# Three merge gates of a hybrid encoder layer, computed among the recurrent branch's first products instead of beside attention

## The chip, the cores and the metric

The kernel runs on one core of a Trainium2 chip. Its engines are TensorE (PE, with its weight loads shown as PEld), VectorE (DVE), ScalarE (ACT), GpSimd (POOL) and SyncE (SP), each with an instruction stream of its own; semaphores order them. The metric is device time in microseconds of one execution; the comparison is between medians of several executions of the kernel before and after the change. Profiles are of one execution each.

## The reference

A trunk of two layers over 512 positions of width 1024, in float32. Each layer normalises x, projects it once, feeds three token mixers, and merges them with three sets of sigmoid gates:

```python
for i in range(DEPTH):                       # DEPTH = 2
    h = rmsnorm(x, mix_norm[i])
    z = h @ w_in[i]
    u_rnn, u_gelu, c_q, ckv_rope, fq, fk, fv, f_logit, gate_logit = split_columns(z)
    y_a = rglru_branch(u_rnn, u_gelu, ...) @ w_br_a[i]      # conv, gates, scan, times gelu
    y_b = mla_branch(c_q, ckv_rope, ...) @ w_br_b[i]        # low-rank attention, chunk mask
    y_c = fox_branch(fq, fk, fv, f_logit, ...) @ w_br_c[i]  # attention with cumulative log forget gates
    g = jax.nn.sigmoid(gate_logit + gate_b[i]).reshape(B, S, N_BRANCH, D)
    merged = g[:, :, 0] * y_a + g[:, :, 1] * y_b + g[:, :, 2] * y_c
    x = x + merged @ w_o[i]
    hf = rmsnorm(x, ffn_norm[i]) @ w_gate_up[i]
    x = x + (jax.nn.silu(hf[..., :D_FF]) * hf[..., D_FF:]) @ w_down[i]
    pg = jax.nn.sigmoid(rmsnorm(x, ple_norm[i]) @ w_ple_gate[i])
    x = x + pg * (p[i] @ w_ple[i])
return rmsnorm(x, final_norm)
```

The gate logits of branch n are 1024 columns of z, so 8 blocks of 128 columns for each branch. The change concerns the first three blocks of branch 0, whose gates multiply the recurrent branch's output y_a.

## The kernel before

**Products in three parts.** Activations lie transposed, 128 channels on the partitions and 512 positions along the free dimension. Every float32 operand is split into a high and a low float32r half, and `mm3` (L239) adds three matmuls: high by high, high by low, low by high. `dense` (L246) makes one block of 128 output channels: it takes a PSUM bank, runs `mm3` for each 128-row weight tile (8 for a projection from width 1024, 4 from width 512), and then calls an evacuation function.

**The weight stream.** All weights are packed in the order of use in units of four 128x128 tiles. SP loads a unit into one of four raw slots (`_load`, L96); ACT casts the high half (L112) and DVE subtracts the low half (L113) into one of five slots. A unit is split when PE is at most five units away from it.

**Pages and banks.** `pf` is a pool of 20 float32 pages of 128x512, `pr` one of 31 pages for split operands, and there are 8 PSUM banks. Each pool is a list: `take` pops the first free entry, `free` or `give` appends at the end (L52 to L82). The lists are worked through while the program is written down; when a page is taken again, its new writer waits on the chip for the last readers of the old content. Inside each engine the order of instructions is made by a scheduler when the kernel is built; it keeps these dependencies, and starts from the order in which the program is written. One engine runs its instructions in the order so made.

**The norm's late scale.** In the first part of `mix` the products read X, the gained but not yet normalised input, and the evacuation multiplies by `st["r"]`, the inverse norm of each position (`scaled`, L278). Later `renorm` (L691) loads x again, makes the normalised and split pages Xn, and `drop_x` frees X and r.

**The order of a layer's mixer**, in `mix` (L441):

- the four recurrent inputs `ev_u` (L452): scaled, convolved along positions, split into `xcp`;
- `key_and_forget` (L511): one product for MLA's shared rotary key and the forget logits. Two pages `later` hold its work. The forget part goes through DVE, ACT's exp, a polynomial on POOL (L376 to L379), a DMA (L534), a cumulative sum on DVE (L537) and a split (L539); its rows end up in `small`, which every score of the forgetting attention needs;
- four gelu blocks `ev_ug` (L467), two pages each, of which one stays as `gx`;
- the recurrent gates: for each of four blocks t two products of one weight tile each (L655), into two banks, evacuated by `lru_gate` (L638) with three pages r, i and a: two tanh, an exp and a further tanh on ACT, one DVE operation with the conv output, whose page is then free. After the loop the two pages `later` are freed (L663);
- `lru_tail` (L666): four square roots on ACT, ordered behind the last tanh because they need another activation table, then per block on DVE two products, a scan (L677), the gelu product and a split: yA;
- key and query projection of the first head pair of the forgetting attention (L685), and `values` (L608), 96 matmuls into four banks;
- `attention` (L751): for 8 heads times 4 query blocks, scores, softmax, transposes on PE (L830), splits, and the product with V. Between these steps `fill` runs other dense work of a plan, a number of weight tiles per step such that the plan is used up within 8 steps; `drain` (L802) finishes it. The first plan (L974) holds two projections, the `renorm` calls, and three `mg(0, j, yA)`, each a gate (8 tiles) and a branch product (4 tiles), 52 tiles in all.

`gate(n, j, box, X, r)` (L714) is a dense block whose evacuation optionally scales by r, applies tanh with the gate's bias and keeps a page z in `box`; `branch` (L725) later multiplies: (z + 1) times the branch's product. `merge` (L745) runs both.

Of the kernel before, what the change touches and what calls it, by code (L numbers as in the profile page):

```python
# [13 lines left out]
AF = mybir.ActivationFunctionType  # L14
# [3 lines left out]
DEPTH, SEQ, D = 2, 512, 1024  # L18
KD = D // 128
# [8 lines left out]
C_U, C_UG, C_CQ, C_CKV, C_KR, C_FQ, C_FK, C_FV, C_FL, C_G = (  # L28
    0, 512, 1024, 1408, 1664, 1696, 2208, 2720, 3232, 3240)


V_MIX, V_FFN, V_PLE, V_GB, V_CW, V_CB, V_BA, V_BX, V_QN, V_KN, V_BF = (
    0, 8, 16, 24, 48, 64, 68, 72, 76, 79, 81)
# [133 lines left out]
class Trunk:  # L167
# [273 lines left out]
    def mix(self, layer):  # L441
        nc = self.nc
        L, st, X = layer, self.st, self.xp
        pf, pr = self.pf, self.pr
# [22 lines left out]
        def ev_ug(t):  # L467
            def f(b):
                u, q = pf.take(), pf.take()
                self.scaled(u.ap, b, st["r"])  # L470
                self.banks.give(b)
                c1 = float(np.sqrt(2.0 / np.pi))
                self.act(q.ap, u.ap, AF.Square, scale=float(np.sqrt(c1 * 0.044715)))
                self.stt(q.ap, q.ap, c1, u.ap, ALU.add, ALU.mult)
                self.act(q.ap, q.ap, AF.Tanh)
                self.stt(q.ap, q.ap, 1.0, u.ap, ALU.add, ALU.mult)
                u.free()
                gx[t] = q
            return f
# [31 lines left out]
        def key_and_forget():  # L511


            b = self.banks.take()
            for k, x in enumerate(X):
                assert self.w.pos // 4 in PACKED
                wh, _ = self.w.tile(("kf", L, k))
                self.mm(b[:, :], wh, x.h, k == 0, False)
                self.mm(b[0:64, :], wh[:, 0:64], x.l, False, k == KD - 1)
                yield  # L520
            (p, q), f = later, rows_f
            z, t, c, g = p.ap[0:40], p.ap[64:104], p.ap[f], q.ap
            nc.scalar.copy(t, b[64:104, :])
            self.tt(z, b[0:40, :], t, ALU.add)
            self.banks.give(b)
            self.tt(z, z, st["r"].ap[0:40])
            nc.gpsimd.dma_start(g[:, 0:32], z[32:40].rearrange("h (c i) -> h c i", c=16))
            load_trig()
            u, t1, t2, o = (g[:, 32 * i:32 * i + 32] for i in range(4))
            self.ts(u, u, self.v(L, V_BF), None, ALU.add)  # L530
            self.log1p_exp_neg(o, t1, t2, u, nc.gpsimd)
            self.ts(t1, u, 0.0, None, ALU.min)
            self.stt(o, o, -2.0, t1, ALU.mult, ALU.add)
            nc.gpsimd.dma_start(c.rearrange("h (c i) -> h c i", c=16), o)  # L534
            rope(p.ap, p.ap, small.h[0:32], small.l[0:32], slice(0, 32))
            free_trig()
            nc.vector.tensor_tensor_scan(c, self.one[f, 0:1].broadcast_to((HEADS, SEQ)), c, 0.0,  # L537
                                         op0=ALU.mult, op1=ALU.add)
            self.split(small.h[f], small.l[f], c)  # L539

        rows_f = slice(64, 64 + HEADS)
        later = [pf.take(), pf.take()]
        self.run(key_and_forget())
        for t in range(4):
            self.run(self.dense(self.win(L, C_UG + 128 * t), X, ev_ug(t)))


        qp, kp = {}, {}
# [59 lines left out]
        def values(spec, X, rT):  # L608

            V = []  # L610
            bs = [self.banks.take() for _ in range(NT)]
            for k, x in enumerate(X):
                wh, wl = self.w.wide(spec + (k,))
                for j in range(NT):
                    c = slice(j * 128, (j + 1) * 128)
                    self.mm3(bs[j][:, :], x.h[:, c], x.l[:, c], wh, wl, k == 0, k == len(X) - 1)
                    yield
            for j in range(NT):
                g = pr.take()
                V.append(g)  # L620
                dst = g.ap.rearrange("p (h t d) -> p h t d", h=HEADS, t=2)
                src = bs[j].rearrange("p (h d) -> p h d", h=HEADS)
                hi = dst[:, :, 0, :]
                if rT is None:
                    self.split(hi, dst[:, :, 1, :], src)
                else:
                    r = rT[:, j:j + 1]
                    self.act(hi, src, AF.Copy, scale=r)
                    self.stt(dst[:, :, 1, :], src, r, hi.bitcast(F32), ALU.mult, ALU.subtract)
                self.banks.give(bs[j])  # L630
            self.V = V


        yA = [None] * 4
# [20 lines left out]
        for t in range(4):  # L655
            bb = []
            for g in range(2):
                b = self.banks.take()
# [1 line left out]
                self.mm3(b[:, :], wh, wl, xcp[t].h, xcp[t].l, True, True)  # L660
                bb.append(b)
            lru_gate(t)(*bb)
        for p in later:  # L663
            p.free()

        def lru_tail():  # L666

# [17 lines left out]
        k0, q0 = fox_proj(0, X, st["r"])  # L685
        self.run(k0)
        self.run(q0)
        self.run(values(("fv", L), X, rT))
        Xn = [None] * KD

        def renorm(*ks):  # L691

            for k in ks:
                t, p = pf.take(), pr.take()
                nc.gpsimd.dma_start(t.ap, x_dram[k])
                self.stt(t.ap, t.ap, self.v(L, V_MIX + k), st["r"].ap, ALU.mult, ALU.mult)
                self.split(p.h, p.l, t.ap)
                t.free()
                Xn[k] = p
            return  # L700
            yield

        def drop_x():
            for p in X:
                p.free()
            st.pop("r").free()
            return
            yield
# [1 line left out]

        merged = [None] * KD
        out_pages = [None] * KD

        def gate(n, j, box, X=Xn, r=None):  # L714
            def f(b):
                z = pf.take()
                if r is not None:
                    self.scaled(z.ap, b, r)
                self.act(z.ap, b[:, :] if r is None else z.ap, AF.Tanh,
                         bias=self.v(L, V_GB + 8 * n + j), scale=0.5)  # L720
                self.banks.give(b)
                box.append(z)
            return self.dense(self.win(L, C_G + D * n + 128 * j), X, f)

        def branch(n, j, ys, box):  # L725
            name = ("w_br_a", "w_br_b", "w_br_c")[n]
# [18 lines left out]
        def merge(n, j, ys, X=Xn, r=None):  # L745
            box = []
            yield from gate(n, j, box, X, r)
            yield from branch(n, j, ys, box)
# [154 lines left out]
        def fp(p, w, X=Xn, r=None):  # L903
            return (fox_proj(p, X, r)[w], 8)

        def mg(n, j, ys, X=Xn, r=None):
            return (merge(n, j, ys, X, r), 12)

        def free_yA():
# [54 lines left out]
        def done_c():  # L964
            for p in oC:
# [5 lines left out]
        lkv = [(latent(ckv, skv, C_CKV, j), 8) for j in range(2)]  # L971
        tail = chain(gate(2, 2, boxes[2, 2]), gate(2, 3, boxes[2, 3]))
        attention(True, oC, [
            [fp(1, 0, X, st["r"]), (renorm(0, 1), 0), mg(0, 0, yA, X, st["r"]), (renorm(2, 3, 4), 0),  # L974
             mg(0, 1, yA, X, st["r"]), (renorm(5, 6, 7), 0), (drop_x(), 0), fp(1, 1), mg(0, 2, yA)],
            [fp(2, 0), mg(0, 3, yA), mg(0, 4, yA), fp(2, 1), mg(0, 5, yA)],
            [fp(3, 0), mg(0, 6, yA), fp(3, 1)] + lq,
            lkv + [mg(0, 7, yA), (free_yA(), 0), (latent_sums(), 0), gt(2, 0), (latent_norm(), 0),
# [413 lines left out]
```

## Time and profile before

| | before |
|---|---|
| median of 3 runs | 1827.73 us (1827.25 to 1828.02) |
| the profiled execution | 1827.03 us, span 1825.3 us |
| granted TensorE clock, mean | 0.995 |
| weight units loaded | 606 of 256 KB |
| HBM read | 173.98 MB |

The span runs from the first to the last instruction; 1.7 us lie around it. Layer 0's mixer starts near 6 us, its attention near 103 us; layer 1's attention starts near 999 us. In rows of windows, each engine's busy microseconds stand with the number of its instructions in brackets, then the granted clock of TensorE (1.00 is full), the share of DMA engines' time and GB/s. In rows of the timeline, the start, the duration, the engine, the line, the operation and its tiles are given; in square brackets stands the idle time of the engine before it and what released it. Groups of instructions give busy time and the mean duration in ns, and the idle time before them.

### The profile page before, as it was taken

The page shows a single profiled execution, that of the slowest core. Times are in us where ns is not written, and L with a number is a line of the kernel's source. Part 1 is how long each engine was busy: PE and PEld are TensorE (multiplying, and loading weights), DVE is VectorE, ACT ScalarE, POOL GpSimd, SP SyncE. Part 2 cuts the span into 40 slices and gives each one's busy share as a digit, 9 for nine tenths or more (in the row PEclk, how much of TensorE's full clock was granted, in tenths as well). Part 3 has the DMA queues.
Part 4 walks back from the last instruction along what each step waited for, and adds up shares of the span by engine and source line. Part 5 has one row for each costly group of instructions (what it writes and reads, how often), then busy time and mean ns, then how long its engine had stood idle before and what let it go on. Part 6 is the DMA issues. An engine that isn't in the chain of part 4 may idle for free. (4 is left out here: it accounts for less than half of the span.)

```text
span 1825.3 us, 24128 instructions
## 1 busy us (share of the span) xinstructions
PE 1804.1 (99%) x8476; PEld 1502.0 (82%) x8476; DVE 1210.6 (66%) x2421; ACT 817.7 (45%) x1562; POOL 117.0 (6%) x234
## 2 busy tenths in 40 slices
PE   9899999999999999999999999999999999999998
PEld 7678888888888888888887788888888888888887
DVE  7897678866665555444778966888576655553457
ACT  4765556553333333223447655565533333332243
POOL 1230001100000000000103200010000000000000
PEclk9899999999999999999999999999999999999999
DMA  5152223324222232322433322242242322233331
GB/s 189 59 151 82 78 80 116 96 73 139 94 98 94 97 98 98 109 94 98 132 111 122 105 81 82 89 118 85 86 129 92 99 98 96 95 110 99 98 116 47
DMA packets 98827, 184.17 MB, mean 101 GB/s; under 512 B 13553, under 2 KB 14753, under 8 KB 98705
## 3 DMA queue, kind: packets, MB, share of 16 engines
q1 hardware_dynamic: 89280, 162.04, 27.0%
q0 software_dynamic: 8416, 19.45, 3.9%
q8 instruction: 66, 1.08, 0.2%
q10 hardware_dynamic: 1008, 1.14, 0.2%
q14 instruction: 57, 0.46, 0.1%
HBM read 173.98 MB, written 4.21 MB: 98 GB/s over the span
## 5 line engine op out<-in xcount | busy, mean ns | idle before, releaser
L237 PE MATMUL bank<-pr,hl 128*128 128x512 f32 (+1 forms) x6812 | 1600.8, 392 | 7.6 <-ACT pr L233 6.9
L237 PEld LDWEIGHTS bank<-pr,hl 128*128 128x128 f32 (+1 forms) x6812 | 1268.5, 188 | 271.0 <-ACT pr L233 8.6
L112 ACT CAST hl<-raw 128x512 fp32r<-128x512 f32 x590 | 364.2, 618 | 670.3 <-PE bank L237 394.5
L113 DVE TENSOR_TENSOR hl<-raw,hl 128x512 fp32r<-128x512 f32 x590 | 404.3, 685 | 379.8 <-ACT hl L112 361.7
L221 DVE TENSOR_TENSOR pf<-pf 128x512 f32<-128x512 f32 (+3 forms) x235 | 151.1, 651 | 31.8 <-ACT pf L230 29.8
L221 DVE TENSOR_TENSOR pf<-bank,pf 128x512 f32<-128x512 f32 (+3 forms) x198 | 132.9, 676 | 57.3 <-PE bank L237 32.6
L230 ACT ACTIVATE pf<-pf 128x512 f32<-128x512 f32 (+1 forms) x145 | 86.1, 600 | 113.2 <-DVE pf L221 110.5
L237 PE MATMUL bank<-pr 128*128 128x256 f32 (+5 forms) x704 | 120.3, 302 | 3.3 <-ACT pf L230 2.5
L237 PEld LDWEIGHTS bank<-pr 128*128 128x128 f32 (+1 forms) x704 | 102.6, 190 | 13.7 <-ACT pf L230 3.3
L221 DVE TENSOR_TENSOR pr<-pf,pr 128x512 fp32r<-128x512 f32 (+3 forms) x126 | 85.5, 682 | 4.5 <-ACT pr L233 3.1
L230 ACT ACTIVATE pf<-bank,small 128x512 f32<-128x512 f32 (+3 forms) x130 | 68.9, 531 | 37.7 <-DVE small L838 34.8
L233 ACT CAST pr<-pf 128x512 fp32r<-128x512 f32 (+2 forms) x114 | 70.3, 620 | 29.5 <-DVE pf L218 20.3
L855 ACT CAST pth<-bank 128x128 fp32r<-128x128 f32 (+3 forms) x128 | 54.1, 427 | 58.5 <-PE bank L830 52.0
L221 DVE TENSOR_TENSOR ptl<-bank,pth 128x128 fp32r<-128x128 f32 (+3 forms) x128 | 61.7, 485 | 13.8 <-ACT pth L855 9.1
L838 DVE TENSOR_REDUCE small<-bank 128x1 f32<-128x128 f32 (+3 forms) x128 | 61.7, 483 | 7.6 <-PE bank L237 6.5
L237 PE MATMUL bank<-hl,pr 128*128 128x512 f32 x240 | 56.2, 390 | 0.3 <-DVE hl L113 0.3
L830 PE MATMUL bank<-identr,pf 128*128 128x128 f32 x320 | 55.0, 273 | 0.0
L237 PEld LDWEIGHTS bank<-hl,pr 128*128 128x128 f32 x240 | 44.8, 188 | 10.0 <-DVE hl L113 0.7
L225 DVE TENSOR_SCALAR pf<-pf,small 128x128 f32<-128x128 f32 (+3 forms) x128 | 48.6, 383 | 2.7
L230 ACT ACTIVATE pf<-bank,vec 128x512 f32<-128x512 f32 x60 | 41.0, 688 | 14.2 <-PE bank L237 13.8
L830 PEld LDWEIGHTS bank<-identr,pf 128*128 128x128 f32 x320 | 40.1, 140 | 8.2
L218 DVE SCALAR_TENSOR_TENSOR pf<-pf,bank 128x512 f32<-128x512 f32 x48 | 32.6, 683 | 20.8 <-PE bank L237 20.4
(112 smaller groups left out, 793.9 us busy)
## 6 DMA issues: line engine op xcount, KB each, us to landing
raw<-wst SPq DMA_DIRECT2D x606, 256.0 KB, 2.6
pf<-xT POOLq DMA_DIRECT2D x16, 256.0 KB, 3.4
pr<-pr POOLq DMA_DIRECT2D x32, 128.0 KB, 2.6
pf<-xs POOLq DMA_DIRECT2D x16, 256.0 KB, 3.3
pf<-trig POOLq DMA_DIRECT2D x12, 256.0 KB, 3.2
pf<-xT SPq DMA_DIRECT2D x8, 256.0 KB, 5.4
xs<-pf POOLq DMA_DIRECT2D x8, 256.0 KB, 2.7
pf<-pT POOLq DMA_DIRECT2D x4, 256.0 KB, 3.0
```

The lines of the kernel that those rows point to most:

```text
L112: self.nc.scalar.copy(hi, src)
L113: self.nc.vector.tensor_tensor(lo, src, hi.bitcast(F32), op=ALU.subtract)
L218: self.nc.vector.scalar_tensor_tensor(out, a, s, b, op0=op0, op1=op1)
L221: self.nc.vector.tensor_tensor(out, a, b, op=op)
L225: self.nc.vector.tensor_scalar(out, a, s1, None, op0=op0)
L230: return self.nc.scalar.activation(out, a, f, **kw)
L233: self.nc.scalar.copy(hi, src)
L237: self.nc.tensor.matmul(out, a, b, start=start, stop=stop, skip_group_check=True)
L830: nc.tensor.transpose(T[:, c], p2.ap[:, c], self.ident[:, :])
L838: nc.vector.reduce_max(R[t][:, 0:1], S[:, :m], axis=AX.X, negate=True)
L855: self.nc.scalar.copy(hi, src)
```

## The change

Gates 0, 1 and 2 of branch 0 are computed early. Gate 0 follows the second gelu block, gate 1 the fourth, both ahead of the recurrent products; gate 2 stands between the query projection of the first head pair and `values`. All three read X and scale by r; before, gates 0 and 1 did so too, and gate 2 read Xn without a scale. Their pages z are kept in `early` until `branch` uses them, and the plan's three `mg` entries hold only the branch product, 4 tiles in place of 12. The two pages `later` are freed right after `key_and_forget` is written down, ahead of the gelu blocks, and not after the recurrent gates. `gate` itself is moved up unchanged. The order of the weight stream follows.

```diff
+        Xn = [None] * KD
+        def gate(n, j, box, X=Xn, r=None):
+            def f(b):
+                z = pf.take()
+                if r is not None:
+                    self.scaled(z.ap, b, r)
+                self.act(z.ap, b[:, :] if r is None else z.ap, AF.Tanh,
+                         bias=self.v(L, V_GB + 8 * n + j), scale=0.5)
+                self.banks.give(b)
+                box.append(z)
+            return self.dense(self.win(L, C_G + D * n + 128 * j), X, f)
+
         rows_f = slice(64, 64 + HEADS)
         later = [pf.take(), pf.take()]
         self.run(key_and_forget())
+        for p in later:
+            p.free()
+        early = [[], [], []]
+
+        def early_gate(j):
+            self.run(gate(0, j, early[j], X, st["r"]))
+
         for t in range(4):
             self.run(self.dense(self.win(L, C_UG + 128 * t), X, ev_ug(t)))
+            if t % 2:
+                early_gate(t // 2)
...
             lru_gate(t)(*bb)
-        for p in later:
-            p.free()
...
         self.run(k0)
         self.run(q0)
+        early_gate(2)
         self.run(values(("fv", L), X, rT))
...
         def mg(n, j, ys, X=Xn, r=None):
+            if early[j:j + 1]:
+                return (branch(n, j, ys, early[j]), 4)
             return (merge(n, j, ys, X, r), 12)
...
-            [fp(1, 0, X, st["r"]), (renorm(0, 1), 0), mg(0, 0, yA, X, st["r"]), (renorm(2, 3, 4), 0),
-             mg(0, 1, yA, X, st["r"]), (renorm(5, 6, 7), 0), (drop_x(), 0), fp(1, 1), mg(0, 2, yA)],
+            [fp(1, 0, X, st["r"]), (renorm(0, 1), 0), mg(0, 0, yA), (renorm(2, 3, 4), 0),
+             mg(0, 1, yA), (renorm(5, 6, 7), 0), (drop_x(), 0), fp(1, 1), mg(0, 2, yA)],
```

More of the change, by code (lines that the diff above doesn't have):

```diff
@@ L687, in mix @@
         self.run(q0)
+        early_gate(2)
         self.run(values(("fv", L), X, rT))
-        Xn = [None] * KD
         def renorm(*ks):
@@ L712, in mix @@
         out_pages = [None] * KD
[L714 to L723, printed above, removed]
         def branch(n, j, ys, box):
```

## The prediction

> **What bounds the kernel now.** I read the page first, then the windows of each stage, then the timeline of the stretches where TensorE (PE) waits. The page gives the engines' totals and the price of one instruction of each kind the change touches.
>
> ```profile
> span 1825.3 us, 24128 instructions
> ...
> PE 1804.1 (99%) x8476; PEld 1502.0 (82%) x8476; DVE 1210.6 (66%) x2421; ACT 817.7 (45%) x1562; POOL 117.0 (6%) x234
> ...
> L113 DVE TENSOR_TENSOR hl<-raw,hl 128x512 fp32r<-128x512 f32 x590 | 404.3, 685 | 379.8 <-ACT hl L112 361.7
> ...
> L221 DVE TENSOR_TENSOR pf<-bank,pf 128x512 f32<-128x512 f32 (+3 forms) x198 | 132.9, 676 | 57.3 <-PE bank L237 32.6
> ...
> L230 ACT ACTIVATE pf<-bank,vec 128x512 f32<-128x512 f32 x60 | 41.0, 688 | 14.2 <-PE bank L237 13.8
> ```
>
> PE is busy for 1804 of 1825 us. A change that moves PE work without removing any can only win back PE's idle and slow stretches. The windows below give busy time in the order PE, PEld, DVE (VectorE), ACT (ScalarE), POOL, then PE's clock.
>
> ```profile
> 45.00:70.00 25.00, 18.12 (x64) 13.56 (x63) 24.54 (x45) 14.21 (x25) 0.82 (x2) 0.80 0.17 54
> 70.00:85.00 15.00, 15.00 (x68) 12.43 (x67) 9.49 (x15) 14.24 (x23) 7.26 (x18) 1.00 0.25 76
> 85.00:135.00 50.00, 49.39 (x219) 39.91 (x218) 49.37 (x90) 33.59 (x64) 15.36 (x30) 1.00 0.45 137
> 135.00:150.00 15.00, 15.00 (x79) 12.66 (x78) 13.05 (x37) 10.17 (x25) 2.12 (x4) 1.00 0.24 75
> 150.00:420.00 270.00, 270.00 (x1346) 225.75 (x1345) 196.64 (x456) 154.76 (x338) 19.80 (x38) 1.00 0.29 90
> ...
> 970.00:985.00 15.00, 15.00 (x68) 12.43 (x67) 8.66 (x16) 14.39 (x24) 8.36 (x18) 1.00 0.29 90
> 985.00:1035.00 50.00, 46.22 (x203) 36.66 (x202) 49.75 (x92) 32.14 (x61) 15.37 (x30) 1.00 0.42 133
> ```
>
> The reader is to see three things. In layer 0, PE loses time at 45 to 70 us; in layer 1 it loses 3.8 us at 985 to 1035. In both layers DVE is full for 50 us (49.37 and 49.75) from the end of the recurrent gates to the first steps of attention. Before that lies a pocket in which DVE idles, 5.5 us in layer 0 and 6.3 us in layer 1, because ACT is full (14.24 and 14.39 of 15). From 150 us on PE is full and DVE has room.
>
> The timeline of PE shows the large loss, and a plain stretch of the feed-forward part gives PE's pace.
>
> ```profile
> 53.81 0.84 PE L237 MATMUL bank<-pr,hl 128*128 128x512 f32 x3
> 58.45 0.75 PE L237 MATMUL bank<-pr,hl 128*128 128x512 f32 x2 [3.81 <-ACT pr L233]
> 60.42 1.22 PE L237 MATMUL bank<-pr,hl 128*128 128x512 f32 x2 [1.22 <-ACT pr L233]
> 63.49 8.87 PE L237 MATMUL bank<-pr,hl 128*128 128x512 f32 x26 [1.85 <-ACT pr L233]
> ```
>
> ```profile
> 600.00:700.00 100.00, 100.00 (x443) 82.81 (x442) 55.72 (x83) 32.90 (x56) 0.00 (x0) 1.00 0.29 98
> ```
>
> ```profile
> 55.00:60.00 5.00, 0.75 (x2) 0.30 (x2) 5.00 (x10) 1.75 (x5) 0.00 (x0) 0.90 0.26 85
> 60.00:65.00 5.00, 2.73 (x6) 1.68 (x7) 5.00 (x10) 3.40 (x6) 0.00 (x0) 0.50 0.23 73
> ```
>
> One 512-wide matmul costs 100/443 = 0.226 us. The 33 matmuls from 53.81 to 72.36 should take 7.5 us and take 18.4 (without the last one's tail): **10.9 us lost** while the recurrent (RG-LRU) products wait for the split conv outputs. About 2.6 us of it is clock (0.50 at 60 to 65 us).
>
> The Trainium skill (TensorE: Matmul & The Clock Gate, What's actually happening) says that PE's clock halves after an idle window of about 3.4 us; the trace agrees, as the clock fell after the 3.81 us wait. By that rule a new wait of this length costs some 2 us more than its length, an estimate, where I take 1.
>
> **The change part by part.** A gate is 8 weight tiles, so 24 matmuls (24 x 0.226 = 5.4 us of PE), two weight units (two DVE halves of 0.685), one DVE scaling (0.676) and one ACT tanh (0.688). Nothing of the sum of PE, ACT or the weight DMAs changes, since 16.3 us of PE per layer only move; the DMA share of 0.23 to 0.26 at 55 to 65 us leaves room for the earlier loads on SP's queue, and no POOL instruction is added. The third gate gains one DVE scaling (0.68 us), because it now reads the unnormed X. Moving the definition costs nothing.
>
> *Layer 0, first products.* Two gates (10.8 us of PE) now fill the wait. PE reaches the recurrent products at 54.5 + 10.8 = 65.3. Their last inputs come from DVE:
>
> ```profile
> 66.42 1.27 DVE L221 TENSOR_TENSOR pr<-pf,pr 128x512 fp32r<-128x512 f32 x2
> ```
>
> That is 67.7 now; four weight halves and two scalings (4.1 us) go in front, so about 71.5 for the products' end. Residual loss 71.5 - 65.3 - 5.4 = 0.8: PE is ahead by **10.1 us** here. In layer 1 PE has no stall at this place, so nothing is gained.
>
> *A new wait.* The two float32 pages of the key-and-forget chain are freed earlier. The free list is first in, first out: 13 pages lie ahead of them, and the two gelu pairs, two gates and the first LRU gate take exactly 2+2+1+2+2+1+3 = 13. So the second LRU gate's tanh (ACT) writes the page in which the forget chain still runs its cumulative sum, and the fourth gate reuses the second one's conv page. Also, eight PSUM banks rotate: with the third gate put in, it gets the bank of that second LRU gate's first product (ten allocations on, modulo eight). So PE's third gate, and values behind it, wait for the tanh, and the tanh for the chain. POOL starts the chain's polynomial here:
>
> ```profile
> 69.82 0.30 POOL L376 TENSOR_SCALAR pf<-pf 128x32 f32<-128x32 f32 x1 [23.91 <-DVE pf L221]
> ```
>
> ```profile
> 81.69 1.22 DVE L537 TENSOR_TENSOR_SCAN pf<-one,pf 8x512 f32<-8x512 f32 x1 [0.98 <-DMA pf<-pf]
> ...
> 85.47 1.31 DVE L218 SCALAR_TENSOR_TENSOR pf<-pf 128x512 f32<-128x512 f32 x2 [0.41 <-ACT pf L230]
> ...
> 88.61 0.68 DVE L221 TENSOR_TENSOR pr<-pf,pr 8x512 fp32r<-8x512 f32 x1
> ```
>
> ```profile
> 983.47 1.22 DVE L537 TENSOR_TENSOR_SCAN pf<-one,pf 8x512 f32<-8x512 f32 x1 [2.85 <-DMA pf<-pf]
> 984.72 1.29 DVE L218 SCALAR_TENSOR_TENSOR pf<-pf 128x512 f32<-128x512 f32 x2
> ```
>
> ```profile
> 83.42 1.28 ACT L230 ACT_TABLE_LOAD   x1
> 84.71 1.95 ACT L230 ACTIVATE pf<-pf,eps 128x512 f32<-128x512 f32 x3
> 86.69 0.61 ACT L233 CAST pr<-pf 8x512 fp32r<-8x512 f32 x1
> ```
>
> The chain ends at 89.3 as run; done at once after the scan (82.9 + 0.6 + 0.7) it would be 84.2. With up to 4.1 us of new DVE work before POOL's start, the bounds are 84.2 and 93; I take 87.0, the prompt end plus two thirds of that work, as the scan's readers have nothing to queue behind once the LRU tail waits too. PE, free for the third gate at 71.5 + 10.8 = 82.3, starts at 87.7 after the tanh: **5.4 us lost**, and 1 of clock. For layer 1 the prompt end is 986.0, and DVE ahead of it holds gates where it held costlier gelu work: 983 to 991, I take 985. Values' 96 matmuls (21.7 us) end at 998.7 there now (the row of the first scores, below), so they start by 977.0, and PE would come to the third gate at 977.0 + 10.8 = 987.8: no wait.
>
> *The LRU tail.* Its square roots come after the last gate's tanh. From the chain's end: three ACT operations (tanh, exp, tanh) at 0.69, the table load of 1.28 and one square root of 1.95/3 = 4.0 us. DVE's tail starts at 91.0 (now 85.5) in layer 0 and at 989.0 (now 984.7) in layer 1.
>
> *Attention's front.* These rows show the first scores, and the first transposes behind them.
>
> ```profile
> 103.48 0.33 PE L237 MATMUL bank<-pr 128*128 128x128 f32 x2
> ```
>
> ```profile
> 135.62 0.27 PE L830 MATMUL bank<-identr,pf 128*128 128x128 f32 x1
> ```
>
> ```profile
> 998.71 0.22 PE L237 MATMUL bank<-pr 128*128 128x128 f32 x1
> ```
>
> ```profile
> 1035.20 1.03 PE L830 MATMUL bank<-identr,pf 128*128 128x128 f32 x8
> ```
>
> PE bridged these 32.1 and 36.5 us with the filler of the first plan: 52 weight tiles of 0.68 us. The change leaves 28, of which, by the bank rotation, 16 (10.9 us) can run before the first transposes. PE would reach attention at 87.7 + 1 + 5.4 + 21.7 (values) = 115.8 and run dry near 129. So **DVE sets the end of this stage**. Its 50 us of full work lose what has moved ahead of the tail: 6 halves and 2 scalings (5.5), the query's evacuation (three of 0.68) and the chain's last subtraction (0.7), 8.2 in all, and gain the new scaling. From the tail's start to the first transposes it is 135.6 - 85.5 = 50.1 us in layer 0 and 50.5 in layer 1. Layer 0: 91.0 + 50.1 - 8.2 + 0.7 = 133.6, against 135.6: **2.0 us early**. Layer 1: 989.0 + 50.5 - 8.2 + 0.7 = 1032.0 against 1035.2: 3.2 early, of which I take **1.5**, since DVE is no longer backlogged to the last and its later steps wait on ACT. Behind this PE is full in both kernels.
>
> Sum: -2.0 - 1.5 = **-3.5 us**. So most of the 10.1 is given back: the filler that covered DVE's backlog is spent. The profiled execution took 1827.03 (span 1825.3 and 1.7 around it), 0.7 under the median of 1827.73; so 1827.03 - 3.5 + 0.7 = 1824.2 as a median.
>
> **The rivals.**
> *All filled.* The chain ends promptly (84.2, and 983 in layer 1) and DVE follows: the tail starts 2.8 and 2 us earlier than I took, so layer 0 gains 4.8 and layer 1 5.2 (nothing withheld): -10.0, 1818. For it: the 10.9 us wait is real, and the chain stands ahead of the gates in program order. Against: DVE is busy 96.5 of the 105 us from 45 to 150, so 8.5 us is the most it can give in layer 0.
>
> *Starved attention (slower).* The scheduler's order keeps the first transposes as far behind the first scores as now, less the 8.2 us moved: first scores at 115.8 and 1015.0 (998.7 + 16.3), transposes at 139.7 and 1043.3, 4.1 and 8.1 late: +12, 1840; half of it 1834. For it: 32.1 and 36.5 us in both layers, at all times with DVE full. Against: values' evacuation and the tail, which filled part of it, will be done earlier. It decides once the first transposes come later than 135.6 and 1035.2.
>
> *ScalarE blocked.* If the waiting tanh stands ahead of the next weight casts, PE runs dry after the three units cast ahead (of five slots two are the recurrent products' own; 12 tiles, 8.2 us): from 79.7 to 87.7 in layer 0, with 2.7 us of products left before the third gate: +2.7, and about as much clock: near 1828 to 1830. The Trainium skill (TensorE: Matmul & The Clock Gate, Architectural detail) says that ScalarE's queue is strictly first in, first out, which is what this rival needs; ACT's order is not known before the build.
>
> *The order does not change.* The scheduler could leave the gates' products behind the recurrent ones: 1828 to 1830.
>
> **How the numbers follow.** Forecast 0.42 (1821 to 1828), all filled 0.24, starved attention 0.20, ScalarE blocked 0.10, order unchanged 0.04. About 0.2% (3.7 us) is what a measurement of this kernel can tell from no change. Faster: all filled and 0.12 of the forecast's edge, 0.36. Same: 0.30 of the forecast, 0.06 and 0.02 of the last two, 0.38. Slower: 0.20 + 0.04 + 0.02 = 0.26. The range reaches from a little past all filled, 1816.5, to short of full starvation, 1837; cases of both signs hold most of the chance, and the forecast's own range is 1821 to 1828.
>
> **What would show it.** Right: no wait of PE over 1 us before the recurrent products in layer 0, clock 1.00 at 55 to 65 us; a wait of 3 to 8 us behind the first query projection, released by ACT; scans of the LRU tail about 5 us later in both layers; PE gaps in attention's first steps. Wrong: no wait at the third gate (then the chain was prompt), first transposes under 131 or over 138 us, or ACT casts late behind a tanh.

## The result and the profile after

The changed kernel takes **1837.96 us** as a median of 6 runs (1836.62 to 1838.50), the kernel before 1827.88 in the same session (1827.25 to 1831.33). The ratio is 1.0053 with a 95% interval of 1.0043 to 1.0064: slower by about 10 us, where 3.5 us faster was forecast, and a little outside the range (1837.0). The profiled execution took 1838.46 us.

The profile page of the changed kernel, with the rows that answer to those of before:

```profile
span 1836.7 us, 24122 instructions
...
PE 1808.6 (98%) x8476; PEld 1507.7 (82%) x8476; DVE 1214.2 (66%) x2423; ACT 817.8 (45%) x1562; POOL 115.9 (6%) x234
```

The work is the same: PE still has 8476 matmuls, ACT 1562 instructions, and DVE's two further instructions (2423 for 2421) are the third gate's scaling, one per layer. The span is 11.4 us longer, so it is the order that costs. The windows of the same stretches as before:

```profile
45.00:70.00 25.00, 25.00 (x112) 20.67 (x112) 25.00 (x45) 15.31 (x28) 0.63 (x1) 1.00 0.24 77
70.00:85.00 15.00, 15.00 (x68) 12.43 (x67) 9.53 (x19) 10.79 (x18) 6.85 (x17) 1.00 0.38 121
85.00:135.00 50.00, 38.62 (x157) 30.19 (x155) 44.97 (x71) 33.48 (x54) 16.06 (x31) 0.90 0.36 112
135.00:150.00 15.00, 14.34 (x66) 11.85 (x67) 12.70 (x39) 8.19 (x25) 1.94 (x4) 0.89 0.17 55
150.00:420.00 270.00, 270.00 (x1345) 225.93 (x1345) 200.73 (x467) 156.87 (x346) 19.32 (x37) 1.00 0.29 88
...
1035.00:1050.00 15.00, 12.04 (x50) 9.88 (x50) 13.41 (x38) 9.12 (x25) 1.94 (x4) 0.77 0.21 69
```

PE is full from 45 to 85 us where it had run 64 matmuls in 25 us and now runs 112, and then starves: 157 matmuls from 85 to 135 us in place of 219, at a mean clock of 0.90. In layer 1 it starves as well (12.04 of 15 us at clock 0.77). From 150 us on it is full, as before.

The layers' shares can be read from the timeline of PE at the last norm ahead of layer 1's mixer, where PE sums squares with a vector of ones (below: the norm sum). Before, and after:

```profile
924.53 0.95 PE L237 MATMUL bank<-one,pf 128*128 128x1 f32 x8
```

```profile
930.66 0.95 PE L237 MATMUL bank<-one,pf 128*128 128x1 f32 x8
```

Layer 0 costs 6.1 us, so layer 1 5.3 of the 11.4. Every later time of layer 1 below is 6.1 us late before layer 1 begins.

**The first gain is there.** PE's timeline after shows one run of matmuls through the place where 10.9 us were lost:

```profile
49.80 26.45 PE L237 MATMUL bank<-pr,hl 128*128 128x512 f32 x116
```

**The page wait is there.** ACT's timeline (start, duration, line, operation; in brackets the idle time before and its releaser):

```profile
87.38 0.69 ACT L230 ACTIVATE pf<-bank,vec 128x512 f32<-128x512 f32 x1 [4.11 <-DMA pf<-pf]
88.55 0.61 ACT L233 CAST pr<-pf 8x512 fp32r<-8x512 f32 x1 [0.47 <-DVE pf L537]
89.27 1.40 ACT L230 ACTIVATE pf<-bank,vec 128x512 f32<-128x512 f32 x2
...
91.43 1.12 ACT L112 CAST hl<-raw 128x512 fp32r<-128x512 f32 x2
...
93.81 1.28 ACT L230 ACT_TABLE_LOAD   x1
95.11 1.95 ACT L230 ACTIVATE pf<-pf,eps 128x512 f32<-128x512 f32 x3
...
99.49 1.12 ACT L112 CAST hl<-raw 128x512 fp32r<-128x512 f32 x2
```

A recurrent gate's tanh at 87.38 waits 4.11 us for a DMA that reads the forget chain's page, and two more tanh come behind the chain's last steps (89.27). The table load that must follow the last of them is 10.4 us later than before (93.81 for 83.42), and after the casts of 91.43 no weight is cast for 7 us. The Trainium skill (TensorE: Matmul & The Clock Gate, Architectural detail) says that ScalarE takes its queue strictly in order; the 4.11 us in which no later instruction ran agree. PE feels it in two waits:

```profile
82.67 8.32 PE L237 MATMUL bank<-hl,pr 128*128 128x512 f32 x36
90.83 5.64 PE L237 MATMUL bank<-pr,hl 128*128 128x512 f32 x24
100.14 2.08 PE L237 MATMUL bank<-hl,pr 128*128 128x512 f32 x4 [3.67 <-ACT hl L112]
105.13 7.07 PE L237 MATMUL bank<-hl,pr 128*128 128x512 f32 x22 [2.91 <-DVE hl L113]
```

The scheduler has put 36 matmuls of the values ahead of the third gate (x24), so PE does not wait there. It waits for weights behind it, 3.67 and 2.91 us; the second wait is for a DVE half that queues with the late LRU tail.

**Then attention's front is short of work.** The same timeline up to the first transposes:

```profile
135.66 4.59 PE L237 MATMUL bank<-pr,hl 128*128 128x512 f32 x12 [2.98 <-ACT pf L230]
...
140.26 1.50 PE L838 MATMUL bank<-identr,pf 128*128 128x128 f32 x12
```

Windows from the first scan of the LRU tail to the first transposes, before and after, say which engine sets this length:

```profile
89.33:135.62 46.29, 45.68 (x203) 36.77 (x201) 45.93 (x85) 29.93 (x58) 15.36 (x30) 1.00 0.48 145
```

```profile
98.89:140.26 41.37, 31.75 (x120) 24.83 (x121) 41.15 (x76) 25.62 (x49) 12.27 (x24) 0.84 0.39 122
```

DVE is 99% busy in both (45.93 of 46.29, 41.15 of 41.37). Before, PE was as busy as DVE. After, DVE still needs 41 us, and PE has 120 matmuls for it in place of 203.

### The profile page after: what moved, and what is told of

Its sections match the earlier page's. It is cut to its first block, busy times and chain, and to the rows that moved or that the text cites. A ratio compares the mean times of both kernels' runs of the same rounds, so it can differ in the third digit from the quotient of the medians.

```text
span 1836.7 us, 24122 instructions
## 1 busy us (share of the span) xinstructions
PE 1808.6 (98%) x8476; PEld 1507.7 (82%) x8476; DVE 1214.2 (66%) x2423; ACT 817.8 (45%) x1562; POOL 115.9 (6%) x234
## 4 chain that ended last, share of the span: by engine, by line
PE 95%; DVE 3%; issue 0%; POOL 0%; ACT 0%; DMA 0%; DVEq 0%; POOLq 0%; ACTq 0%
PE bank L237 93%; PE bank L838 2%; DVE pf L218 1%; DVE pr L221 1%; DVE hl L113 0%; DVE pr L218 0%; DVE pf L696 0%; DVE pf L221 0%; POOL pf L378 0%; ACT pf L230 0%; POOL pf L379 0%; DMA pf<-pf 0%; DVE bank L221 0%; DVE small L218 0%; ACT L230 0%
## 5 line engine op out<-in xcount | busy, mean ns | idle before, releaser
L230 ACT ACTIVATE pf<-pf 128x512 f32<-128x512 f32 (+2 forms) x145 | 86.1, 600 | 113.9 <-DVE pf L221 110.5
L237 PEld LDWEIGHTS bank<-pr 128*128 128x128 f32 (+1 forms) x704 | 103.3, 191 | 10.9 <-DVE pf L221 1.7
L233 ACT CAST pr<-pf 128x512 fp32r<-128x512 f32 (+2 forms) x114 | 69.9, 619 | 23.7 <-DVE pf L218 14.6
L221 DVE TENSOR_TENSOR ptl<-bank,pth 128x128 fp32r<-128x128 f32 (+3 forms) x128 | 61.6, 485 | 15.4 <-ACT pth L863 11.5
```

The lines of the kernel that those rows point to most:

```text
L221: self.nc.vector.tensor_tensor(out, a, b, op=op)
L230: return self.nc.scalar.activation(out, a, f, **kw)
L233: self.nc.scalar.copy(hi, src)
L237: self.nc.tensor.matmul(out, a, b, start=start, stop=stop, skip_group_check=True)
```

## The experiments

Two causes stand against each other: **W**, the page wait, and **F**, the 24 weight tiles (16.3 us of PE) per layer that attention's first plan lacks. All kernels were run several times, each beside the kernel before (medians 1827.4 to 1827.8 us in these sessions).

| kernel | median, us | ratio to before, 95% interval |
|---|---|---|
| nowait | 1826.43 | 0.9992 (0.9983 to 1.0002) |
| refill | 1825.80 | 0.9988 (0.9979 to 0.9998) |
| nowait_refill | 1818.81 | 0.9946 (0.9931 to 0.9961) |
| later_alone | 1833.50 | 1.0028 (1.0018 to 1.0039) |
| third_late | 1838.82 | 1.0060 (1.0045 to 1.0075) |
| two | 1847.88 | 1.0110 (1.0095 to 1.0125) |
| two_x | 1842.96 | 1.0083 (1.0068 to 1.0098) |
| nr_two | 1836.05 | 1.0044 (1.0029 to 1.0059) |
| nr_third_late | 1818.11 | 0.9948 (0.9931 to 0.9964) |
| cand_x | 1822.31 | 0.9970 (0.9957 to 0.9982) |
| cand_more | 1816.66 | 0.9939 (0.9924 to 0.9953) |
| before_refill | 1826.45 | 0.9991 (0.9982 to 1.0000) |

### The page wait taken away: nowait

```diff
-        for p in later:
-            p.free()
+        zz = pr.take()
...
-            self.run(gate(0, j, early[j], X, st["r"]))
+            self.run(gate(0, j, early[j], X, st["r"], (zz.h, zz.l, None)[j]))
...
             lru_gate(t)(*bb)
+        for p in later:
+            p.free()
```

> The changed kernel, with the two pages of the key-and-forget chain freed after the recurrent gates as before; room for the first two early gates is found in one split page, so their z is kept rounded to float32r. No gate's tanh then waits for the chain; the filler moved out of attention's first plan stays moved. Theory W (the page wait): the tanh that waits 4.11 us holds the weight casts behind it, and the 10.5 us that PE loses from 96 to 109 us of layer 0 come from that, as do some 3.7 of the 14.7 us by which layer 1's square roots are later. Without the wait 1838.0 - 10.5 - 3.7 = about 1824 us, and ACT shows no wait over 1 us at a DMA from 70 to 110 us. Theory F (the filler): attention's first plan has 28 weight tiles in place of 52, 16.3 us of PE that no longer bridge the way from the first scores to the first transposes. The time stays at 1834 to 1839; what is not lost before attention is lost inside its first eight steps, and the first transposes stay near 140 and 1044 us.

Measured: 1826.43 us, 11.5 under the changed kernel, and level with the kernel before. ACT's timeline:

```profile
86.70 1.95 ACT L230 ACTIVATE pf<-pf,eps 128x512 f32<-128x512 f32 x3
...
89.81 0.62 ACT L233 CAST pr<-pf 8x512 fp32r<-8x512 f32 x1
```

The chain itself is no faster (its split's cast at 89.81, after 88.55 in the changed kernel); the square roots simply do not stand behind it any more, and start 8.4 us earlier (86.70 for 95.11). Layer 0 is 6.1 us shorter (norm sum at 924.56 for 930.66) and layer 1 as much, though in layer 1 of the changed kernel no ACT instruction waits for the chain's DMA: there the tanh only stand behind the chain in ACT's order. The time is 2.4 us above W's figure and 7.6 below F's. But F is not gone. PE now waits inside attention's first steps, at clock 0.50 behind both waits (12 matmuls in 5.49 us where 2.7 are usual):

```profile
119.03 5.49 PE L237 MATMUL bank<-pr,hl 128*128 128x512 f32 x12 [3.21 <-DVE pr L218]
...
128.44 4.55 PE L237 MATMUL bank<-pr,hl 128*128 128x512 f32 x12 [2.97 <-ACT pf L230]
```

So without the wait the change is worth nothing: what is won at the recurrent products is lost here.

### The first plan filled again: refill

```diff
-             ..., (drop_x(), 0), fp(1, 1), mg(0, 2, yA)],
-            [fp(2, 0), mg(0, 3, yA), mg(0, 4, yA), fp(2, 1), mg(0, 5, yA)],
-            [fp(3, 0), mg(0, 6, yA), fp(3, 1)] + lq,
-            lkv + [mg(0, 7, yA), (free_yA(), 0), ...
+             ..., (drop_x(), 0), fp(1, 1), mg(0, 2, yA), mg(0, 3, yA), mg(0, 4, yA)],
+            [fp(2, 0), mg(0, 5, yA), mg(0, 6, yA), fp(2, 1), mg(0, 7, yA), (free_yA(), 0)],
+            [fp(3, 0), fp(3, 1)] + lq,
+            lkv + [...
```

> The changed kernel, with two merges (gate and branch, 24 weight tiles) moved up from the second plan of the forgetting attention into its first, so that this plan has 52 tiles again; the later plans move up by two merges. Theory F: the 7.4 and 10.8 us that PE loses in attention's first steps fall back to about 1.5 and 4.9, so 1838.0 - 11.8 = about 1826 us, if the later plans do not run short in turn (then the loss shows up behind 150 us). Theory W: the page wait and the late casts at 96 to 109 us are still there, 1835 to 1838 us, with the first transposes near 140 us.

Measured: 1825.80 us, 12.2 under the changed kernel, as F had it. The page wait and the waits for weights are all still there, as W had it for the rest:

```profile
99.81 1.20 PE L237 MATMUL bank<-hl,pr 128*128 128x512 f32 x4 [3.67 <-ACT hl L112]
104.79 14.61 PE L237 MATMUL bank<-hl,pr 128*128 128x512 f32 x56 [3.79 <-DVE hl L113]
...
140.13 0.49 PE L838 MATMUL bank<-identr,pf 128*128 128x128 f32 x3
```

The first transposes come at 140.13, where the changed kernel has them at 140.26, and layer 0 is nevertheless 6.4 us shorter (its norm sum at 924.23). The date of the first transposes is not the price; what PE has to do until then is. The later plans pay little back: behind 150 us the largest new wait is 1.06 us, once in each layer (near 270 and 1167 us).

### Both: nowait_refill

It has both diffs above.

> Both at once: no page wait, and the first plan filled again with two merges of the second. If the two causes add, 1838.0 - 14.2 - 11.8 = about 1812 us; if theory W alone is right about 1824, if theory F alone about 1826. If the kernel is bound by the way from the recurrent gates to the first transposes on DVE and ACT, whatever PE does meanwhile, the first transposes stay at 133 us or later and the time between 1820 and 1830.

Measured: 1818.81 us, 19.2 under the changed kernel: not the full sum of 23.7, for the two causes share one stretch. Each covers part of the other's loss. With the first plan filled, the page wait costs 1825.80 - 1818.81 = 7.0 us, with the short plan 11.5. Without the page wait, the filler is worth 1826.43 - 1818.81 = 7.6 us, with it 12.2. The window of layer 0 from the tail's first scan to the first transposes:

```profile
93.04:134.46 41.42, 39.39 (x170) 32.10 (x169) 41.20 (x71) 25.07 (x46) 15.24 (x30) 0.96 0.46 148
```

DVE is as full as in the other kernels, in the same length (41.4 us), but PE now has 170 matmuls for it. The third alternative, that DVE and ACT alone set the time, falls with its 1820 to 1830 us, if only by 1.2, though the transposes do stay past 133 us.

### One line of the change alone: later_alone

```diff
         self.run(key_and_forget())
+        for p in later:
+            p.free()
...
             lru_gate(t)(*bb)
-        for p in later:
-            p.free()
```

> The kernel before, with the one line of the change that frees the two pages of the key-and-forget chain ahead of the gelu blocks; no gate is moved and every plan is as before. By the order of the page list the second recurrent gate's exp then writes a page that the chain still uses. Theory W: ACT waits some 3 to 5 us behind it, casts come late, and the time is 1831 to 1834 us. Theory F: no filler is moved, so 1827 to 1829 us.

Measured: 1833.50 us, 5.9 over the kernel before (1827.64 in that session) and inside W's figures. A tanh waits, where an exp was expected, for 2.72 us in layer 0 (below) and 3.56 in layer 1, where 3 to 5 were expected:

```profile
82.73 0.69 ACT L230 ACTIVATE pf<-bank,vec 128x512 f32<-128x512 f32 x1 [2.72 <-DMA pf<-pf]
```

The line that was needed to make room for the early gates costs 5.9 us by itself as a difference of medians (5.1 by the ratio of 1.0028), about half of it in each layer (layer 0's norm sum is at 927.55, so 3.0 there).

### The control: before_refill

> The kernel before, with two merges of the second plan moved up into the first (76 tiles), no gate early and no page freed early. It is the control for the fastest kernels: the refilled plan can win at most what PE loses in attention's first steps of the kernel before, about 1.1 us in layer 0 and 4.9 in layer 1, and nothing of the 10.9 us at the recurrent products: 1823 to 1828 us. Under 1822 would say that the early gates are not what wins there.

Measured: 1826.45 us, 0.9 under the kernel before (1827.37), within what was expected. The edit is that of refill, in the kernel before. Moving merges forward alone wins next to nothing, so the early gates are what makes 1818.8 us possible: with the refilled plan and no page wait they are worth 1826.45 - 1818.81 = 7.6 us, against the 10.1 us of the forecast's first step.

### Where the third gate stands: third_late, two, two_x

`third_late` exchanges two lines of the changed kernel:

```diff
-        early_gate(2)
         self.run(values(("fv", L), X, rT))
+        early_gate(2)
```

> The changed kernel, with the third early gate behind the values' product and not ahead of it; page wait and short first plan are as in the changed kernel. Theory B (the bank): the third gate waits for the PSUM bank of the second recurrent gate, and while it waits its two weight units hold two of the five slots, so the values behind it run out of weights; with it behind the values the 10.5 us lost at 96 to 109 us fall to about 3, and the time is 1829 to 1833 us. Theory C (ScalarE's order): the casts are late because they stand behind the waiting tanh and the square roots on ACT, wherever the third gate is; PE still loses 8 to 11 us among the values and the time is 1836 to 1840 us.

Measured: 1838.82 us. Theory B falls, and the time is theory C's. PE's waits for weights are shorter (2.71 and 1.46 us), but the front of attention takes the difference back: before the first transposes, at 140.28 us, it waits 4.25 us where the changed kernel waited 2.98.

`two` leaves the third gate in the plan, as before the change:

```diff
-        early_gate(2)
...
-        early = [[], [], []]
+        early = [[], []]
```

> The changed kernel without its third early gate: gates 0 and 1 stay among the recurrent products, the third goes back into attention's first plan, which then has 36 tiles. The page wait stays. Theory B: no gate waits for a bank, so the 10.5 us go, and a third of the filler is back (some 4 us of 11.8): 1824 to 1828 us. Theory C: the wait stays on ACT and only the filler's third is won: 1832 to 1836 us.

Measured: 1847.88 us, a miss of both theories by over 10 us: with eight more tiles in the plan the kernel is 9.9 us *slower* than the changed one. PE's timeline in layer 1:

```profile
1041.52 0.80 PE L237 MATMUL bank<-pr,hl 128*128 128x512 f32 x1 [6.00 <-ACT pr L233]
1044.76 6.49 PE L237 MATMUL bank<-pr,hl 128*128 128x512 f32 x19 [2.44 <-ACT pf L230]
1051.09 0.82 PE L837 MATMUL bank<-identr,pf 128*128 128x128 f32 x6
```

PE waits 6.00 us for a renormed block Xn (L233 is its split), and the first transposes stand behind that wait. The plan's third gate reads Xn; the early one had read X. If that is the cause, a tile bridges only when its inputs are there. `two_x` tests it: the third gate in the plan reads X, ahead of the last `renorm`.

```diff
-             mg(0, 1, yA), (renorm(5, 6, 7), 0), (drop_x(), 0), fp(1, 1), mg(0, 2, yA)],
+             mg(0, 1, yA), (gate(0, 2, x2, X, st["r"]), 8), (renorm(5, 6, 7), 0), (drop_x(), 0),
+             fp(1, 1), (branch(0, 2, yA, x2), 4)],
```

> The kernel with two early gates and the third in attention's first plan (1847.9 us), with that third gate reading X and scaled by r, as gates 0 and 1 did in the kernel before, so that it stands ahead of the last renormed blocks; the weight tiles are the same. Theory R (readiness): a plan's tile only bridges if its inputs are there; on the normalised blocks the gate waits for DVE's and ACT's renorm work and holds up attention's steps behind it on PE. On X it is ready, and the time comes back to that of the changed kernel or below, 1833 to 1839 us, with PE's waits on ACT's renorm split (3.3 and 6.0 us) gone. Theory O: moving the gate to the front of attention's plan is itself what costs (fewer tiles ahead of the first scores); it stays at 1845 to 1849 us.

Measured: 1842.96 us: half of the 9.9 us comes back, and the time lies between the two theories' figures. Readiness is not shown as the cause. The waits on ACT's renorm split are gone from layer 0, but layer 0 is only 0.6 us shorter (norm sum at 934.20 for 934.85). In layer 1 PE still waits almost as long at the same place, now for another ACT instruction:

```profile
1041.35 7.44 PE L237 MATMUL bank<-pr,hl 128*128 128x512 f32 x25 [5.64 <-ACT pf L230]
```

Why the third gate costs so much in the plan was not settled.

### Beyond both kernels: nr_two, nr_third_late, cand_x, cand_more

All four build on nowait_refill. `nr_two` leaves the third gate in the plan and moves one merge there in place of two (48 tiles):

```diff
-        early_gate(2)
...
-             mg(0, 3, yA), mg(0, 4, yA)],
+             mg(0, 3, yA)],
```

> The kernel without the page wait and with the first plan filled again (1818.8 us), less its third early gate, which goes back into the first plan; one merge of the second plan follows it there, so that the plan has 48 tiles. If the third gate's place costs anything of its own, this is 1 to 3 us faster, 1816 to 1818 us; if only the tiles in front of the first transposes count (the third gate gives 8 ahead of attention, and the plan is 4 shorter here), it is 1 to 3 us slower, 1820 to 1822 us.

Measured: 1836.05 us, 17.2 us slower, where 1 to 3 us in either direction were expected. Two things change at once. Twelve tiles fewer per layer are computed ahead of the second plan's start (2 x 12 x 0.68 = 16.3 us of PE), and the third gate reads Xn inside the plan again, which in `two` cost 9.9 us although no tile went behind the second plan's start. How the 17.2 us divide between the two is not shown. It is no general price of a tile: the 24 tiles per layer that `refill` moved in (2 x 24 x 0.68 = 32.6 us) won 12.2 us, and the 24 of `before_refill` 0.9.

`nr_third_late` moves the third gate behind the values, as above:

> The kernel without the page wait and with the first plan filled again (1818.8 us), with its third early gate behind the values. The same products stand ahead of attention in another order. Theory C and the pages: no wait is left that the order could bring forward or hide, so 1817.5 to 1820 us. Theory B: the gate's bank is free by then in both, the same. A difference of over 2 us would say that DVE's order among the values' evacuation and the gate matters: the gate's scaling and tanh then fall between the values' splits and the first scores.

Measured: 1818.11 us, the same.

`cand_x` starts from it and lets the second key and query projection read X:

```diff
              mg(0, 0, yA), (renorm(2, 3, 4), 0),
-             mg(0, 1, yA), (free_zz(), 0), (renorm(5, 6, 7), 0), (drop_x(), 0), fp(1, 1), mg(0, 2, yA),
+             fp(1, 1, X, st["r"]), mg(0, 1, yA), (free_zz(), 0), (renorm(5, 6, 7), 0), (drop_x(), 0), mg(0, 2, yA),
```

> The kernel without the page wait, with a refilled plan and the third gate behind the values (1818.1 us), with the second key and query projection reading X with its scale instead of the normalised blocks, ahead of the last renormed ones. Theory R: PE's wait of 2.1 us behind the renorm work in layer 0 and the half clock after it (1.6 us) go, for two DVE scalings (1.4 us) per layer: 1814 to 1817 us. If DVE's full stretch alone sets the end, the added scalings are all that counts: 1819 to 1821 us.

Measured: 1822.31 us, 4.2 slower and above both figures. Its windows:

```profile
85.00:130.00 45.00, 45.00 (x203) 37.32 (x201) 42.99 (x71) 29.78 (x52) 15.39 (x31) 1.00 0.38 131
130.00:140.00 10.00, 4.02 (x14) 2.54 (x13) 9.90 (x23) 5.77 (x13) 0.00 (x0) 0.78 0.23 79
```

The wait near 122 us is gone, as theory R said, and PE is full up to 130 us. Then it has spent what it had and idles while DVE is full (9.90 of 10). The idle time has moved and grown.

`cand_more` moves a third merge of the second plan into the first (64 tiles, then 40):

```diff
-             mg(0, 3, yA), mg(0, 4, yA)],
-            [fp(2, 0), mg(0, 5, yA), mg(0, 6, yA), fp(2, 1), mg(0, 7, yA), (free_yA(), 0)],
+             mg(0, 3, yA), mg(0, 4, yA), mg(0, 5, yA)],
+            [fp(2, 0), mg(0, 6, yA), fp(2, 1), mg(0, 7, yA), (free_yA(), 0)],
```

> The same kernel (1818.1 us), with a third merge moved from the second plan into the first (64 tiles, then 40). If DVE's full stretch is still longer than the tiles that are ready, 12 more win some of the 4 to 5 us that PE still loses in layer 0: 1814 to 1817 us. If the added tiles all come behind the last wait, or the second plan runs short instead, it stays at 1817.5 to 1821 us.

Measured: **1816.66 us**, ratio 0.9939, the fastest and within the first figure; its interval overlaps that of nr_third_late. Both beat the kernel before by about 10 us.

## Why the prediction was wrong

**The first step was right.** PE is ahead by 81.72 + 48 x 0.226 - 82.67 = 9.9 us when the values start (their first matmul after is the row at 82.67 above; that of before follows); forecast 10.1. (The products' end was put at 71.5; its own terms, 67.7 + 4.1, give 71.8 and so 9.8. Of the 10.9 us lost before the change, the three waits shown make 6.9, so the slow clock's part was about 4.0 and not 2.6; the sum does not use it.)

```profile
81.72 8.55 PE L237 MATMUL bank<-hl,pr 128*128 128x512 f32 x37
```

**The page wait was right in kind.** A recurrent tanh waits for the forget chain, by the page that the free list named. Where PE would stop was wrong: the scheduler put values ahead of the third gate, and PE stopped behind it, for weights that ACT cast late. That is the rival "ScalarE blocked", listed at 0.10, at a higher price than the 2.7 us and "about as much clock" that it was given: from 96 to 110 us PE runs 21 matmuls, 4.7 us of work, so 9.3 us are lost.

```profile
96.00:110.00 14.00, 7.42 (x21) 5.10 (x19) 13.94 (x21) 9.11 (x15) 2.73 (x5) 0.63 0.34 105
```

**Two terms of the tail were too small.** DVE's timeline of the changed kernel has the chain's last subtraction and the tail's first operation:

```profile
89.27 0.68 DVE L221 TENSOR_TENSOR pr<-pf,pr 8x512 fp32r<-8x512 f32 x1
...
95.86 1.31 DVE L218 SCALAR_TENSOR_TENSOR pf<-pf 128x512 f32<-128x512 f32 x2 [1.79 <-ACT pf L230]
```

The chain ends at 89.95, where 87.0 was taken ("the prompt end plus two thirds of that work"; within its bounds): 2.9 us. The chain starts late and then runs promptly. POOL begins 6.1 us after the 69.82 of before, where "up to 4.1" was allowed for, and waits for DVE until then:

```profile
75.89 0.79 POOL L376 TENSOR_SCALAR pf<-pf 128x32 f32<-128x32 f32 x1 [29.00 <-DVE pf L221]
```

From the chain's end to the tail it takes 5.9 us for the 4.0 of "three ACT operations, the table load and one square root", since weight casts and a head's cast go between: 1.9 us. The same two DVE rows of layer 1:

```profile
990.03 0.68 DVE L221 TENSOR_TENSOR pr<-pf,pr 8x512 fp32r<-8x512 f32 x1
...
996.74 1.30 DVE L218 SCALAR_TENSOR_TENSOR pf<-pf 128x512 f32<-128x512 f32 x2 [2.59 <-ACT pf L230]
```

Less layer 0's 6.1 the chain ends at 984.6 here, where 985 was taken, and the tail starts at 990.6 for 989.0, so 6.0 us after it, again for 4.0.

**"DVE sets the end of this stage" was right. The step that failed is the sum that follows it, which took a layer's gain to be the shift of its first transposes.** A layer ends at that date plus the PE work that is left behind it. The date was forecast too early, and the work left was taken to be the same in both kernels, so the removed filler had no price beyond the date at which PE "runs dry".

- *The date.* Beside the two terms above, DVE's stretch from the tail's start to the transposes took 44.4 us in layer 0 for the 42.6 forecast, and 47.2 in layer 1 for the 44.7 left after what was withheld. DVE was busy for 44.18 and 46.22 us of it, where the sum left 42.2 and 42.7 of the 49.73 and 50.23 before (less 8.2, plus 0.7). So more DVE work stayed in the stretch than the sum left there; which work it is was not followed up.
- *The work left.* "Behind this PE is full in both kernels" held. The windows run from the first transposes to the norm sum, before, after, and in `refill`:

```profile
135.62:924.53 788.91, 788.91 (x3656) 655.93 (x3655) 497.92 (x967) 329.95 (x638) 35.01 (x66) 1.00 0.31 100
```

```profile
140.26:930.66 790.40, 790.40 (x3663) 657.24 (x3662) 499.29 (x971) 330.74 (x641) 34.94 (x66) 1.00 0.31 100
```

```profile
140.13:924.23 784.10, 782.93 (x3626) 650.08 (x3625) 499.39 (x976) 329.57 (x643) 35.67 (x68) 1.00 0.30 100
```

After the change 1.5 us more of work are left in layer 0. PE had starved ahead of the transposes, and 7 matmuls more come behind them. In `refill` the transposes come hardly earlier, 4.5 us later than before the change, but 6.3 us less is left behind them, and layer 0 ends 0.3 us earlier than before the change (924.23 for 924.53). Filling the plan is worth 12.2 us with the page wait and 7.6 without: this term the sum had put at nothing.

From -2.0 the four terms of layer 0 give -2.0 + 2.9 + 1.9 + 1.8 + 1.5 = 6.1. In layer 1 the same terms are -0.4, 2.0, 2.5 and, as the rest, 2.7: from -1.5 to +5.3. So of the 14.9 us between forecast and profile, 6.4 lie in the chain and the tail behind it, 4.3 in DVE's stretch and 4.2 in the work left behind the transposes.

These shares say where the time appeared, not what would bring it back. `nowait` kept the short plan and won 11.5 us; `refill` kept the late transposes and won 12.2. Without the page wait the time is 1826.4, inside the forecast's own range, which had the wait in it, so that agreement would have been luck; the 1818 of "all filled" needed the refilled plan too.

**The rival "starved attention"** had the result in its span (1834 to 1840), with the first transposes at 139.7 for 140.26 measured in layer 0. Its working was not what happened: the first scores came at 119.75, not 115.8, and the distance to the transposes shrank by 11.6 us rather than 8.2. Its layer 1 figure, 1043.3, meets the measured 1043.93 only because that contains layer 0's 6.1 us. "All filled" and "the order does not change" are out. Of the named signs these came true: no stall at the recurrent products, scans of the LRU tail late (by 9.6 us in layer 0 for about 5), gaps in attention's first steps, transposes past 138, casts late behind a tanh. PE did not wait at the third gate either, which was to say that the chain was prompt; it was not, the gate had only been put behind 36 other matmuls.

Not settled: how the page wait's cost divides between the late tail and the late casts, which come from the same tanh, and why the third gate costs what it does in the plan (`two`, `two_x`, `nr_two`).

## What to carry to other kernels

Where two engines are full in the same stretch, filler moved forward out of it is not free: ask how long the slower engine will still need and which tiles the other has left for that time, and move later filler up in the same edit. A page freed early to make room hands its next writer a wait on its old readers; follow the free list to that writer, then down its engine's queue to what stands behind it. A single date such as the first transposes says when a stage's engine is done, not what the stage costs: the work left behind it counts too.

## What the runs showed of the hardware

PE's clock fell after shorter waits than the 3.81 us of the kernel before. In nowait_refill PE was full until 122 us and waited 2.03 us, until 124.48. The clock was still 1.00 then, fell while PE was at work again, and was back at 1.00 by 129 us:

```profile
122.00:124.00 2.00, 0.45 (x2) 0.02 (x1) 2.00 (x5) 1.09 (x2) 0.00 (x0) 1.00 0.22 85
124.00:125.00 1.00, 0.52 (x2) 0.48 (x3) 1.00 (x3) 0.34 (x2) 0.00 (x0) 1.00 0.23 55
125.00:126.00 1.00, 1.00 (x4) 0.72 (x4) 1.00 (x3) 0.86 (x4) 0.00 (x0) 0.72 0.55 207
126.00:127.00 1.00, 1.00 (x4) 0.80 (x3) 1.00 (x3) 0.99 (x2) 0.00 (x0) 0.50 0.10 27
127.00:128.00 1.00, 1.00 (x4) 0.81 (x3) 1.00 (x3) 0.95 (x3) 0.00 (x0) 0.50 0.68 234
128.00:129.00 1.00, 1.00 (x4) 0.78 (x4) 1.00 (x4) 1.00 (x3) 0.16 (x1) 0.58 0.25 55
```

If the clock was either 1.00 or 0.50, these means give 0.56 + 1 + 1 + 0.84 = 3.4 us at half clock, so about 1.7 us lost, an estimate. In cand_more a wait of 1.76 us did the same (27 matmuls in 8.17 us where 6.1 are usual):

```profile
123.58 8.17 PE L237 MATMUL bank<-pr,hl 128*128 128x512 f32 x27 [1.76 <-DVE pf L221]
```

But the kernel before waited 2.24 us at 1021 to 1023 us and kept clock 1.00:

```profile
1021.00:1023.00 2.00, 0.00 (x0) 0.00 (x0) 1.97 (x5) 1.97 (x5) 0.15 (x1) 1.00 0.08 25
1023.00:1025.00 2.00, 1.93 (x8) 1.59 (x9) 1.94 (x4) 1.61 (x5) 1.12 (x3) 1.00 0.46 131
```

The Trainium skill (TensorE: Matmul & The Clock Gate, What's actually happening) puts the drop behind an idle window of about 3.4 us and calls the window free-running. Drops after waits of 2.03 and 1.76 us do not fit the 3.4 us as it was read for the prediction; the measurement decides. In this kernel one should count on the drop from a wait of about 1.8 us on, not always, and on about 1.7 us of cost beside the wait.
